# Matrix products that read their moving operand in turns of four columns from each 64-byte line, and a tile of ones 32 bytes lower

## The chip, the cores and the metric

The kernel runs on one core of a Trainium2 chip. The metric is the device time of one execution in microseconds (us), median of the runs shown. Besides these times there is one profiled execution; all rows below come from it.

## The reference

One decoder block in float32 over 256 tokens of width 2048: a mixer with gated linear attention (4 heads) beside multi-scale pooling, merged by sigmoid gates, then cross-attention into 256 memory tokens, then a gated MLP with a depthwise convolution of width 3 (inner width 5632), each on an RMS-normed input and added to the residual stream; at the end a last RMS norm.

```
x = x + hybrid_mixer(rms_norm(x, g_mix), w_in, ..., w_branch, w_out)
x = x + memory_cross_attention(rms_norm(x, g_cross), rms_norm(mem, g_mem), w_cq, w_ckv, w_co)
x = x + conv_glu_ffn(rms_norm(x, g_ffn), w_up, conv_w, conv_b, w_down)
return rms_norm(x, g_final)
```

## The kernel before

**Layout.** Activations lie with features on the 128 partitions and tokens along the free axis. A chunk of 128 features by 256 tokens is held as two float32r parts, the rounded value (hi) and the rest (lo). Class `Act` keeps two chunks in a tile of 4096 bytes per partition: 256 columns hi and 256 columns lo of the first chunk, then the same of the second. `act.both(c)` is the 512 columns of chunk c, `act.hi(c)` its first 256.

**Weights.** They come from DRAM in units (a half unit is up to 1024 columns), and each half is split into hi (`wh`, written by ScalarE) and lo (`wl`, written by VectorE, L110). Both are kept three units ahead of their use.

**Products.** A block of 128 output features is made by `products` from pairs of matmuls into one PSUM tile of 512 columns, 16 pairs in most units:

- L321 multiplies with `wh` all 512 moving columns (hi and lo of the tokens);
- L322 multiplies with `wl` the 256 hi columns and adds into the first half of the same PSUM tile.

Each of the two has a weight load of its own, 128 columns. `total` or `residual` adds the halves of the PSUM tile afterwards. Nearly all products of the kernel go this way: 56 units of `w_in` (tiles ps_k, ps_q, ps_r, ps_g, ps_p), 16 each of `w_branch` (br), `w_out` (ps_wo), the keys (ps_ck), `w_cq` (ps_cq) and `w_co` (ps_wc), 88 of `w_up` (ps_up), 32 of `w_down` with 16 pairs (ps_dn), 10 with 12 pairs (ps_dl), and the first pair of each of the last 6 (ps_dt). That is 56 x 16 + 80 x 16 + 88 x 16 + 32 x 16 + 10 x 12 + 6 = 4222 pairs.

**Other products**, not by `products`: the values and decay inputs at the start (va, L395 to L397), the cross-attention's values (cv, L713 to L715), scores (cs) and outputs (co), and the last six units of `w_down` after their first pair (L912, L913, L918), which read the moving columns as two runs of 128. Plain float32 products stand between: the attention levels (sc, L513), whose moving operand is read in runs of 1, 2, 4, ... up to 64 columns; sums over partitions (cps, L270, one moving column of `ones`); and spreads over partitions with `ones` as the weights (rps, L279, 256 moving columns, and oss, L579, 512).

**Where tiles lie.** The pools follow each other in each partition's memory; two padding pools of 192 and 64 bytes stand around the pool of `wh`. In the built program all `Act` tiles begin at 160 modulo 256 bytes, `wl` at 160, `wh` at 96, `ones` at 192, `ident` at 192.

**Order.** Each engine runs its instructions in the program's order; TensorE's weight loads run beside its matmuls.

Of the kernel before, what the change touches and what calls it, by code (L numbers as in the profile page):

```python
# [8 lines left out]
F32 = mybir.dt.float32  # L9
# [6 lines left out]
P = 128  # L16
T = 256
# [125 lines left out]
def block(ctx, tc, xT, memT, vecs, masks, wa2, wpool, w_va, w_in, w_branch, w_out, w_ckv_k, w_ckv_v, w_cq, w_co, w_up, w_down, out):  # L143
    nc = tc.nc
    PS = bass.MemoryType.PSUM
    const = ctx.enter_context(tc.tile_pool(name="const", bufs=1))
# [63 lines left out]
    nc.sync.dma_start(vec[:, V_CB:], vecs[:, V_CB:])  # L210
    eps_t = const.tile([P, 1], F32, name="eps_t")
    nc.vector.memset(eps_t, EPS)
    ones = const.tile([P, P], F32, name="ones")
    ident = const.tile([P, P], F32, name="ident")
    nc.vector.memset(ones, 1.0)
    make_identity(nc, ident)
    scrap = const.tile([P, 1], F32, name="scrap")
# [5 lines left out]
    pe = {}  # L223
# [83 lines left out]
    def gemm(unit, act, name, n=NC):  # L307

        ps = mm.tile([P, 2 * T], F32, tag="mm", name=f"ps_{name}")
        products(ps, terms(W.get(unit), act, n))  # L310
        return ps

    def terms(wps, act, n):
        return [(wps[2 * k // n], k % (n // 2), act, k) for k in range(n)]

    def products(ps, terms, first=True, last=True):
        for i, ((hi, lo), k, act, c) in enumerate(terms):
            f = first and i == 0
            l = last and i == len(terms) - 1
            wh, wl = hi[:, k * P : (k + 1) * P], lo[:, k * P : (k + 1) * P]  # L320
            nc.tensor.matmul(ps, lhsT=wh, rhs=act.both(c), start=f, stop=False, skip_group_check=True)  # L321
            pe["last"] = nc.tensor.matmul(ps[:, 0:T], lhsT=wl, rhs=act.hi(c), start=False, stop=l, skip_group_check=True)  # L322

    def start_pair(units, act, name, n=NC, between=()):

        wps = [W.get(u) for u in units]
        pss = [mm.tile([P, 2 * T], F32, tag="mm", name=f"ps_{name}{i}") for i in range(2)]
        for half in range(2):
            for i in range(2):
                products(pss[i], terms(wps[i], act, n)[half * n // 2 : (half + 1) * n // 2], first=half == 0, last=half == 1)  # L330
                for f in between[2 * half + i : 2 * half + i + 1]:
                    behind(f)
        return pss
# [318 lines left out]
    for m in range(NC):  # L652
        wps = W.get(br0 + m)
        ys = []
        for n in (1, 0):
            ps = mm.tile([P, 2 * T], F32, tag="mm", name=f"br{m}_{n}")
            products(ps, [(wps[n], k, og if n == 0 else op, k) for k in range(8)])
            y = total(ps, f"br{m}_{n}")
            nc.vector.scalar_tensor_tensor(y, gates[m // 2][:, m % 2, n, :], 1.0, y, ALU.add, ALU.mult)
            ys.append(y)  # L660
        nc.vector.tensor_add(ys[0], ys[0], ys[1])
        nc.scalar.mul(mg.hi(m), ys[0], 0.5)
        nc.vector.scalar_tensor_tensor(mg.lo(m), ys[0], 0.5, mg.hi(m).bitcast(F32), ALU.mult, ALU.subtract)
# [27 lines left out]
    for m in range(NC):  # L691
        ps = gemm(ck0 + m, me, f"ck{m}")
# [10 lines left out]
    for g in range(4):  # L703
        acc = [mm.tile([P, 512], F32, tag="mm", name=f"cv{g}_{t}") for t in range(2)]
        for j in range(4):
            wps = W.get(cv0 + 4 * g + j)
            for k in range(4):
                hi, lo = wps[k // 2]
                wh, wl = hi[:, (k % 2) * 512 : (k % 2 + 1) * 512], lo[:, (k % 2) * 512 : (k % 2 + 1) * 512]
                c = 4 * j + k  # L710
# [82 lines left out]
    last = []  # L793
# [112 lines left out]
    for m in range(NC - TAIL, NC):  # L906
        pool, tag = (aux, "aux") if m >= NC - 2 else (mm, "mm")
        ps = pool.tile([P, 2 * T], F32, tag=tag, name=f"ps_dt{m}")
# [69 lines left out]
```

## Time and profile before

| | |
|---|---|
| time, median of 3 runs | 1702.03 us (1701.56 to 1702.17) |
| time of the profiled execution | 1702.15 us |
| its span, first to last instruction | 1700.4 us |
| TensorE matmuls busy | 1689.0 us, 99% of the span |
| TensorE weight loads busy | 1490.3 us, 88% |
| VectorE, ScalarE busy | 1228.0 us (72%), 897.2 us (53%) |
| mean granted TensorE clock | 0.998 |

Busy time of a matmul includes its way through the array, during which the next has already begun; the pace is therefore read from the starts of successive matmuls, not from their durations.

### The profile page before, as it was taken

The page shows a single profiled execution, that of the slowest core. Times are in us where ns is not written, and L with a number is a line of the kernel's source. Part 1 is how long each engine was busy: PE and PEld are TensorE (multiplying, and loading weights), DVE is VectorE, ACT ScalarE, POOL GpSimd, SP SyncE. Part 2 cuts the span into 40 slices and gives each one's busy share as a digit, 9 for nine tenths or more (in the row PEclk, how much of TensorE's full clock was granted, in tenths as well). Part 3 has the DMA queues.
Part 4 walks back from the last instruction along what each step waited for, and adds up shares of the span by engine and source line. Part 5 has one row for each costly group of instructions (what it writes and reads, how often), then busy time and mean ns, then how long its engine had stood idle before and what let it go on. Part 6 is the DMA issues. An engine that isn't in the chain of part 4 may idle for free.

```text
span 1700.4 us, 25992 instructions
## 1 busy us (share of the span) xinstructions
PE 1689.0 (99%) x9900; PEld 1490.3 (88%) x9900; DVE 1228.0 (72%) x1904; ACT 897.2 (53%) x1376; POOL 31.7 (2%) x137
## 2 busy tenths in 40 slices
PE   9999999999999999999999999999999999999997
PEld 9988988888888888889988888888888888888887
DVE  7687658667889755447777788775677776567776
ACT  7555456445556544445555655553355554345564
POOL 2000000000001000000000000000000000000000
PEclk9999999999999999999999999999999999999999
DMA  8665556556666566655446665666665566665563
GB/s 276 193 204 166 174 161 208 182 169 196 192 218 218 184 191 188 186 186 167 152 148 191 189 190 190 187 186 187 190 190 188 186 187 188 190 191 186 170 178 112
DMA packets 90734, 316.15 MB, mean 186 GB/s; under 512 B 10208, under 2 KB 11104, under 8 KB 90608
## 3 DMA queue, kind: packets, MB, share of 16 engines
q1 hardware_dynamic: 90464, 314.43, 59.4%
q8 instruction: 77, 1.26, 0.3%
q14 instruction: 49, 0.40, 0.1%
q10 hardware_dynamic: 144, 0.05, 0.0%
HBM read 312.35 MB, written 2.10 MB: 185 GB/s over the span
## 4 chain that ended last, share of the span: by engine, by line
PE 99%; DMA 0%; DVE 0%; SPq 0%; ACT 0%; issue 0%; DVEq 0%; ACTq 0%
PE ps_up L321 19%; PE ps_up L322 10%; PE ps_dn L321 7%; PE ps_g L321 7%; PE ps_dn L322 4%; PE ps_ck L321 3%; PE ps_g L322 3%; PE ps_wc L321 3%; PE ps_wo L321 3%; PE ps_cq L321 3%; PE br L321 3%; PE cv L714 2%; PE ps_ck L322 2%; PE cv L713 2%; PE cv L715 2%; PE ps_p L321 2%
## 5 line engine op out<-in xcount | busy, mean ns | idle before, releaser
L110 DVE TENSOR_TENSOR wl<-raw,wh 128x1024 fp32r<-128x1024 f32 (+3 forms) x602 | 718.1, 1194 | 379.4 <-ACT wh L110 371.9
L110 ACT CAST wh<-raw 128x1024 fp32r<-128x1024 f32 (+3 forms) x602 | 614.6, 1023 | 712.2 <-issue 273.2
L321 PE MATMUL ps_up<-h,wh 128*128 128x512 f32 x1408 | 493.0, 395 | 0.0
L322 PE MATMUL ps_up<-h,wl 128*128 128x256 f32 x1408 | 394.8, 280 | 0.0
L321 PEld LDWEIGHTS ps_up<-h,wh 128*128 128x128 f32 x1408 | 264.7, 188 | 61.1
L322 PEld LDWEIGHTS ps_up<-h,wl 128*128 128x128 f32 x1408 | 264.3, 188 | 0.0
L321 PE MATMUL ps_dn<-ga,wh 128*128 128x512 f32 x512 | 179.3, 395 | 0.0
L321 PE MATMUL ps_g<-h,wh 128*128 128x512 f32 x512 | 178.0, 394 | 0.0
L322 PE MATMUL ps_dn<-ga,wl 128*128 128x256 f32 x512 | 143.6, 280 | 0.0
L322 PE MATMUL ps_g<-h,wl 128*128 128x256 f32 x512 | 142.1, 277 | 0.0
L321 PEld LDWEIGHTS ps_dn<-ga,wh 128*128 128x128 f32 x512 | 96.3, 188 | 22.3
L321 PEld LDWEIGHTS ps_g<-h,wh 128*128 128x128 f32 x512 | 96.2, 188 | 20.7 <-ACT wh L110 0.2
L322 PEld LDWEIGHTS ps_g<-h,wl 128*128 128x128 f32 x512 | 96.2, 188 | 0.3 <-issue 0.2
L322 PEld LDWEIGHTS ps_dn<-ga,wl 128*128 128x128 f32 x512 | 96.1, 188 | 0.0
L321 PE MATMUL ps_ck<-me,wh 128*128 128x512 f32 x256 | 89.7, 395 | 0.0
L321 PE MATMUL ps_cq<-h,wh 128*128 128x512 f32 x256 | 87.8, 390 | 0.0
L321 PE MATMUL ps_wc<-oc,wh 128*128 128x512 f32 x256 | 87.6, 390 | 0.0
L321 PE MATMUL ps_wo<-mg,wh 128*128 128x512 f32 x256 | 87.3, 389 | 0.0
L322 PE MATMUL ps_ck<-me,wl 128*128 128x256 f32 x256 | 71.7, 280 | 0.0
L322 PE MATMUL ps_cq<-h,wl 128*128 128x256 f32 x256 | 70.7, 276 | 0.0
L322 PE MATMUL ps_wc<-oc,wl 128*128 128x256 f32 x256 | 70.5, 276 | 0.0
L322 PE MATMUL ps_wo<-mg,wl 128*128 128x256 f32 x256 | 70.5, 276 | 0.0
(321 smaller groups left out, 2765.5 us busy)
## 6 DMA issues: line engine op xcount, KB each, us to landing
raw<-w_up SPq DMA_DIRECT2D x176, 512.0 KB, 3.6
raw<-w_in SPq DMA_DIRECT2D x112, 512.0 KB, 3.9
raw<-w_down SPq DMA_DIRECT2D x64, 512.0 KB, 3.6
raw<-w_branch SPq DMA_DIRECT2D x32, 512.0 KB, 4.4
raw<-w_out SPq DMA_DIRECT2D x32, 512.0 KB, 4.4
raw<-w_ckv_k SPq DMA_DIRECT2D x32, 512.0 KB, 3.7
raw<-w_ckv_v SPq DMA_DIRECT2D x32, 512.0 KB, 3.5
raw<-w_cq SPq DMA_DIRECT2D x32, 512.0 KB, 4.3
```

The source lines that it names most:

```text
L110: return self.nc.scalar.copy(hi, src), self.nc.vector.tensor_sub(lo, src, hi.bitcast(F32))
L321: nc.tensor.matmul(ps, lhsT=wh, rhs=act.both(c), start=f, stop=False, skip_group_check=True)
L322: pe["last"] = nc.tensor.matmul(ps[:, 0:T], lhsT=wl, rhs=act.hi(c), start=False, stop=l, skip_group_check=True)
L713: nc.tensor.matmul(acc[t], lhsT=xh, rhs=wh, start=c == 0, stop=False)
L714: nc.tensor.matmul(acc[t], lhsT=xh, rhs=wl, start=False, stop=False)
L715: nc.tensor.matmul(acc[t], lhsT=xl, rhs=wh, start=False, stop=c == NC - 1)
```

## The change

`products` hands both matmuls views of the same memory in another order. `fours` splits the 512 (or 256) columns into 64-byte lines of 16 columns, and each line into four groups of four columns. The matmul goes first through the first group of every line, then the second group of every line, and so on: four columns (16 bytes), a jump of 64 bytes from group start to group start, 32 (or 16) groups in one turn, four turns. PSUM is written in the same order, so each result lands where it did.

The second part puts a gap of 224 bytes ahead of `ones` and one of 32 bytes behind it. `ones` then begins at 160 modulo 256, everything behind it moves by 256 bytes, so all other tiles keep their place modulo 256.

```
+    gaps = [const.tile([P, 56], F32, name="gap0")]
     ones = const.tile([P, P], F32, name="ones")
+    gaps.append(const.tile([P, 8], F32, name="gap1"))
     ident = const.tile([P, P], F32, name="ident")
+    for gap in gaps:
+        nc.vector.memset(gap, 0.0)
...
+    def fours(ap):
+
+        return ap.rearrange("p (l u e) -> p u l e", u=4, e=4)
+
     def products(ps, terms, first=True, last=True):
...
-            nc.tensor.matmul(ps, lhsT=wh, rhs=act.both(c), start=f, stop=False, skip_group_check=True)
-            pe["last"] = nc.tensor.matmul(ps[:, 0:T], lhsT=wl, rhs=act.hi(c), start=False, stop=l, skip_group_check=True)
+            nc.tensor.matmul(fours(ps), lhsT=wh, rhs=fours(act.both(c)), start=f, stop=False, skip_group_check=True)
+            pe["last"] = nc.tensor.matmul(fours(ps[:, 0:T]), lhsT=wl, rhs=fours(act.hi(c)), start=False, stop=l, skip_group_check=True)
```

No instruction changes its place on any engine. On TensorE the 4222 x 2 matmuls of `products` have the shape 128x4x32x4 in place of 128x512, or 128x4x16x4 in place of 128x256; VectorE has two small memsets more.

## Rows read from the trace of the kernel before

**Rows 1.** The page: span, busy time, clock and DMA by slices, chain by engine.

```profile
span 1700.4 us, 25992 instructions
...
PE 1689.0 (99%) x9900; PEld 1490.3 (88%) x9900; DVE 1228.0 (72%) x1904; ACT 897.2 (53%) x1376; POOL 31.7 (2%) x137
...
PEclk9999999999999999999999999999999999999999
DMA  8665556556666566655446665666665566665563
...
PE 99%; DMA 0%; DVE 0%; SPq 0%; ACT 0%; issue 0%; DVEq 0%; ACTq 0%
```

**Rows 2.** Timeline of TensorE, queries of the cross-attention: start, duration, instruction.

```profile
800.11 0.39 PE L321 MATMUL ps_cq<-h,wh 128*128 128x512 f32 x1
800.34 0.28 PE L322 MATMUL ps_cq<-h,wl 128*128 128x256 f32 x1
800.45 0.39 PE L321 MATMUL ps_cq<-h,wh 128*128 128x512 f32 x1
800.68 0.28 PE L322 MATMUL ps_cq<-h,wl 128*128 128x256 f32 x1
800.79 0.39 PE L321 MATMUL ps_cq<-h,wh 128*128 128x512 f32 x1
```

**Rows 3.** Timeline of TensorE, the MLP's first product.

```profile
1000.05 0.40 PE L321 MATMUL ps_up<-h,wh 128*128 128x512 f32 x1
1000.28 0.28 PE L322 MATMUL ps_up<-h,wl 128*128 128x256 f32 x1
1000.40 0.40 PE L321 MATMUL ps_up<-h,wh 128*128 128x512 f32 x1
```

**Rows 4.** Windows: length; busy (instructions) of PE, PEld, DVE, ACT, POOL; clock, DMA share, GB/s.

```profile
251.00:323.00 72.00, 72.00 (x414) 63.00 (x413) 54.42 (x87) 41.92 (x63) 0.25 (x2) 1.00 0.63 198
...
395.00:570.00 175.00, 174.99 (x1030) 154.52 (x1029) 152.00 (x238) 103.50 (x176) 11.99 (x14) 1.00 0.64 205
583.00:660.00 77.00, 77.00 (x443) 67.47 (x441) 44.75 (x57) 31.82 (x40) 0.00 (x0) 1.00 0.61 188
962.00:1623.00 661.00, 661.00 (x3778) 578.75 (x3778) 489.61 (x734) 342.24 (x496) 8.63 (x86) 1.00 0.61 186
```

**Rows 5.** Timeline of TensorE around the spread of the norms in the keys.

```profile
580.75 0.39 PE L321 MATMUL ps_ck<-me,wh 128*128 128x512 f32 x1
...
581.09 0.39 PE L321 MATMUL ps_ck<-me,wh 128*128 128x512 f32 x1
581.32 0.28 PE L322 MATMUL ps_ck<-me,wl 128*128 128x256 f32 x1
581.43 0.59 PE L279 MATMUL rps_mem<-diag_mem,ones 128*128 128x256 f32 x2
581.87 0.59 PE L279 MATMUL rps_wo<-diag_wo,ones 128*128 128x256 f32 x2
...
582.65 0.40 PE L321 MATMUL ps_ck<-me,wh 128*128 128x512 f32 x1
...
583.00 0.40 PE L321 MATMUL ps_ck<-me,wh 128*128 128x512 f32 x1
```

**Rows 6.** The chain that ended last, in order of time: start, length, what.

```profile
120.67 1.73 PE sc L513 x16
...
196.87 1.73 PE sc L513 x16
...
248.61 1.72 PE oss L579 x4
323.13 1.73 PE pps L616 x8
...
961.98 0.43 PE rps_wc L279 x2
1629.51 0.57 PE ps_dl L321 x2
```

**Rows 7.** Timeline of TensorE, scores of the cross-attention.

```profile
860.09 0.28 PE L742 MATMUL cs<-ka,qa 128*128 128x256 f32 x1
860.21 0.28 PE L740 MATMUL cs<-ka,qa 128*128 128x256 f32 x1
860.33 0.28 PE L741 MATMUL cs<-ka,qa 128*128 128x256 f32 x1
```

**Rows 8.** Timeline of TensorE, sums over partitions, one moving column each.

```profile
575.07 0.50 PE L270 MATMUL cps_mem<-ones,acc_mem 128*128 128x1 f32 x4
575.43 0.58 PE L270 MATMUL cps_wo<-ones,acc_wo 128*128 128x1 f32 x4
575.88 0.47 PE L321 MATMUL ps_ck<-me,wh 128*128 128x512 f32 x1
```

**Rows 9.** Timeline of TensorE, the last units of the MLP's second product.

```profile
1670.63 0.28 PE L912 MATMUL ps_dt<-ga,wl 128*128 128x256 f32 x1
1670.75 0.28 PE L913 MATMUL ps_dt<-ga,wh 128*128 128x256 f32 x1
1670.87 0.28 PE L912 MATMUL ps_dt<-ga,wl 128*128 128x256 f32 x1
```

## Prediction

> **What bounds the kernel now.** The page comes first. TensorE is busy for 99% of the span, the chain that ended last is TensorE for 99%, and its granted clock is full in every slice [rows 1]. Nothing else has to become quicker for a gain, and nothing is late: what counts is the pace of the matmuls themselves.
>
> That pace is read from the timeline, from start to start. In the cross-attention's queries a pair of `products` begins every 0.34 us: 0.23 for the 512 columns, 0.11 for the 256 [rows 2]. In the MLP it is 0.35: 0.23 and 0.12 [rows 3]. At the granted clock of 1.00, which is 2.4 GHz, 768 columns are 768 / 2.4 = 320 ns. So each pair loses 20 or 30 ns, with nothing waited for.
>
> The windows show that these are two settled paces. From 395 to 570 us 515 pairs take 175 us, 0.340 each; from 962 to 1623 us 1889 pairs take 661 us, 0.350 each; the windows at 251 and 583 give 0.348 [rows 4]. Same instructions, same shapes, same clock, two paces. What switches them is seen in the keys: pairs at 0.34, then four plain float32 records with `ones` as the weights, and from there on pairs at 0.35 [rows 5]. The chain names the other two such places and their ends [rows 6]: the spread of the attention norms at 248.61 (with `ones`), until the pooling products at 323.13; the spread for the MLP at 961.98, until two products wait at 1629.51. So the longer pace holds 72.8 us from 250.3 to 323.1, 78.3 us from 582.6 to the end of the keys near 661, and 667.1 us from 962.4 to 1629.5: 818 us, or 818 / 0.350 = 2338 of the 4222 pairs.
>
> I read this as two streams of one engine that fall into step. While the moving columns of one matmul run, the weights of the next are loaded from the same memory, and how the two stand to each other decides the loss. Three rows bear this out. Scores of 256 moving columns, with moving operand and weights both at 160 modulo 256, take 0.12 each [rows 7], though the 256 columns of a pair with the next `wh` at 96 take 0.11 at the better pace: same columns, other offsets. Products with one moving column stand 0.81 us for eight records, 0.10 each [rows 8]: that is about what a weight load alone costs, so a 256-column matmul cannot go below it. And plain float32 products, which take the moving columns at half the rate, lose next to nothing: two records with 256 columns take 0.44 us [rows 5], 0.22 each for 512 steps, of which 512 / 2.4 = 0.213.
>
> The Trainium skill, "TensorE: Matmul & The Clock Gate", Part 2, step 1, says the two read ports are independent and loading the next weights takes nothing from the running matmul. By that, the two paces should not exist; the rows above differ, and the measurement decides.
>
> **The change, part by part.** *Tile of ones at 160.* `ones` stands at 192, half a 64-byte line beside the weights of `products` (96 and 160). If the longer pace is entered through `ones` for that reason, `ones` at 160 leaves the pairs at the shorter pace: 2338 x (350 - 340) = 23.4 us. Lower bound: nothing, if any float32 spread sets the longer pace. The matmuls with `ones` themselves are a handful of microseconds and keep theirs.
>
> *The turns, number of instructions.* 4222 pairs before and after, in the same order; weight loads unchanged; no wait added; no DMA moved. VectorE's two small memsets lie at the start, where TensorE still waits for the first weights; they cost nothing I can see.
>
> *The turns, pace.* No row shows a matmul that reads four columns and jumps, at full rate. Bounds: the best is columns alone, 320 ns a pair, and with the rows for the undisturbed case (about 215 for 512 steps, 110 for the weight load under the 256) 325 to 327. The worst that the nearest rows give is one lost step for each piece. At 0.34 a pair is 816 clocks for 768 columns, which is 17 for each 16: as if each 64-byte line cost one. If each group of four cost one, it would be 5 for 4, 960 clocks, 400 ns. What shows short runs is the attention levels: their moving operand goes in runs of 1 to 64 columns, yet each level takes 1.73 us for 16 records, the first and the last alike [rows 6]; but 64 columns at half rate hide under the weight load's 0.11, so this only says that a jump is not dear there. Two runs of 128 cost as much as one of 256, 0.12 and 0.12 [rows 9].
>
> I take a gain, near the undisturbed end. In order, the moving columns go through a 64-byte line in 16 clocks and keep the same neighbourhood to the weight load for long; in turns they leave a line after four, so the two meet often and briefly rather than for a stretch. Of the 20 ns lost at the shorter pace the undisturbed rows explain 5 to 7; of the other 13 I let the turns remove 9: 331 ns a pair. That share is a choice between the ends.
>
> **Sum.** 4222 x (340 - 331) = 38.0 us, and 23.4 us from the pairs now at 350: 61.4 us. Against the profiled execution's 1702.15 us (span 1700.4 and 1.75 around it; the median is 1702.03) that gives 1640.7, say **1641 us**.
>
> *Cover.* Where TensorE speeds up by 3 to 6%, the others must follow. Between 395 and 570 us VectorE is busy 152 of 175 [rows 4], 87%, and would be 89% at 331 ns; ScalarE stands at 104. In the MLP VectorE has 490 of 661. DMA is at 0.64 at most. So nothing else becomes the bound; if the weights' split were late in the branches, it would be late by a part of the 5 us gained there.
>
> **The rivals.**
>
> *Only the ones count.* The turns leave the 17 clocks for 16 as they are, and all pairs run at 340: 1702.15 - 23.4 = 1679. For it: 544 and 272 clocks at the better pace are in proportion to the columns, as a loss of the moving stream alone would be. Against: 256 columns with other weights lose twice as much [rows 7].
>
> *Neither counts.* The paces are set by something else, the float32 spread itself, and the turns run as before: 1702.
>
> *The poorer step everywhere.* With turns the two streams always fall into the longer pace: the other 1884 pairs lose 10 ns each, 18.8 us: 1721. With the 0.12 and twice that of the scores it would be 360 a pair and 1702 + 1884 x 20 + 2338 x 10 = 1763.
>
> *A jump costs a clock.* On the other side outright: 960 clocks a pair, 1702 + 1884 x 60 + 2338 x 50 = 1932. It decides early: the ones give 23.4 us / 4222 = 5.5 ns a pair on average, and a pair has 192 groups of four, so 0.03 ns more for each group eats it. For it: the 17 for 16. Against: the same count of lines costs once 0.11 and once 0.12, so most of the loss is not the line's.
>
> The Trainium skill speaks for this last rival: "PSUM — Partial Sum Buffer", Specifications, gives PSUM cachelines of 8 bytes and says any access pattern that is not contiguous slows matmuls significantly. The turns write PSUM in pieces of 16 bytes. It gives no size; no row here writes PSUM in such pieces. "SBUF — State Buffer", Specifications, asks for at least two hits in each 16-byte line, which groups of four float32 columns meet.
>
> **How the numbers follow.** Gain of the turns, alone or with the ones (1615 to 1665): 0.45. Only the ones (1665 to 1695): 0.20. Neither: 0.06. Poorer step (1705 to 1763): 0.12. A jump costs (beyond): 0.17. The predicted time is the first case's. About 0.2%, 3.4 us, is what a measurement of this kernel tells from no change: faster 0.65, within 0.06, slower 0.29. The range runs from 1615 (325 ns a pair) to 1721 (all pairs at 350); it leaves out the jump's cost and the dearer part of the poorer step. The likeliest case's own range is 1615 to 1665.
>
> **What the profile would show.** Starts of L329 and L330 (the same two matmuls) in the queries every 0.33 us in place of 0.34, in the MLP the same 0.33, no step at the spreads with `ones`. The windows' share of VectorE should rise. If the queries stay at 0.34 and the MLP comes down to 0.34, only the ones counted. If pairs take 0.36 or more in every stage, the jumps or the meeting of the two streams cost more than the order in line did, and the sign is wrong. If the two paces remain, the reading of the ones is wrong.

## The result: faster by 1.4%, where 3.6% was forecast

The changed kernel takes 1677.74 us (median, 1677.48 to 1679.01) beside 1702.1 us of the kernel before: a ratio of 0.9858, 95% interval 0.9841 to 0.9875. That is 24.4 us less; the forecast was 61.4 us less, 1641 us. The sign and the range (1615 to 1721) held; the size did not.

The page of the changed kernel: span, busy time by engine, granted clock, and the chain that ended last by engine. These lines answer to [rows 1].

```profile
span 1675.7 us, 25994 instructions
...
PE 1663.7 (99%) x9900; PEld 1480.0 (88%) x9900; DVE 1228.0 (73%) x1906; ACT 899.2 (54%) x1376; POOL 31.5 (2%) x137
...
PEclk9999999999999999999999999999999999999999
...
PE 98%; DVE 1%; DMA 0%; issue 0%; SPq 0%; ACT 0%; DVEq 0%; ACTq 0%
```

TensorE is still the bound, its clock is still full (0.998 on average), VectorE's work is the same to a tenth of a microsecond. Nearly all of the 24.7 us of span, 24.3, came off the pace of the pairs. Where, the windows say; they have the columns of [rows 4].

```profile
251.00:323.00 72.00, 72.00 (x423) 63.92 (x422) 55.55 (x90) 42.63 (x65) 0.25 (x2) 1.00 0.63 205
395.00:570.00 175.00, 174.99 (x1030) 155.18 (x1029) 153.16 (x240) 104.88 (x178) 12.95 (x15) 1.00 0.64 205
583.00:660.00 77.00, 77.00 (x447) 67.97 (x446) 45.64 (x57) 33.17 (x42) 0.00 (x0) 1.00 0.63 195
```

From 395 to 570 us 1030 matmuls ran before and 1030 run now: the pairs that stood at 0.340 us stand there still. The window at 251 us holds 423 matmuls in place of 414. Start by start, the MLP and the keys after their spread with `ones` (timeline of TensorE; [rows 3] and [rows 5] are the same places):

```profile
999.95 0.39 PE L329 MATMUL ps_up<-h,wh 128*128 128x512 f32 x1
1000.18 0.28 PE L330 MATMUL ps_up<-h,wl 128*128 128x256 f32 x1
1000.29 0.39 PE L329 MATMUL ps_up<-h,wh 128*128 128x512 f32 x1
1000.52 0.28 PE L330 MATMUL ps_up<-h,wl 128*128 128x256 f32 x1
1000.63 0.39 PE L329 MATMUL ps_up<-h,wh 128*128 128x512 f32 x1
```

```profile
577.95 0.59 PE L283 MATMUL rps_mem<-diag_mem,ones 128*128 128x256 f32 x2
578.38 0.59 PE L283 MATMUL rps_wo<-diag_wo,ones 128*128 128x256 f32 x2
...
579.14 0.39 PE L329 MATMUL ps_ck<-me,wh 128*128 128x512 f32 x1
...
579.49 0.39 PE L329 MATMUL ps_ck<-me,wh 128*128 128x512 f32 x1
...
579.83 0.39 PE L329 MATMUL ps_ck<-me,wh 128*128 128x512 f32 x1
```

A pair begins every 0.34 us where it was 0.35, and after the spread the pace stays. Taken from the starts of all pairs, the median is 340 ns in every stage, 225 for the 512 columns and 115 for the 256; the kernel before had 227 and 113 (or 226 and 114) at its shorter pace, 233 and 117 at its longer. The sum over the pairs is 1438.0 us where it was 1462.3, 24.3 less: 2338 pairs by 10 ns is 23.4. So the pairs at 350 came down to 340, and the pairs at 340 did not move.

### The profile page after: what moved, and what is told of

It is laid out like the page before. It is cut to its first block, busy times and chain, and to the rows that moved or that the text cites. A ratio compares the mean times of both kernels' runs of the same rounds, so it can differ in the third digit from the quotient of the medians.

```text
span 1675.7 us, 25994 instructions
## 1 busy us (share of the span) xinstructions
PE 1663.7 (99%) x9900; PEld 1480.0 (88%) x9900; DVE 1228.0 (73%) x1906; ACT 899.2 (54%) x1376; POOL 31.5 (2%) x137
## 4 chain that ended last, share of the span: by engine, by line
PE 98%; DVE 1%; DMA 0%; issue 0%; SPq 0%; ACT 0%; DVEq 0%; ACTq 0%
PE ps_up L329 19%; PE ps_up L330 10%; PE ps_g L329 7%; PE ps_dn L329 7%; PE ps_g L330 4%; PE ps_dn L330 4%; PE ps_wo L329 3%; PE ps_wc L329 3%; PE ps_cq L329 3%; PE ps_ck L329 3%; PE br L329 3%; PE cv L722 2%; PE cv L721 2%; PE cv L723 2%; PE ps_cq L330 2%; PE ps_wc L330 2%
## 5 line engine op out<-in xcount | busy, mean ns | idle before, releaser
L329 PE MATMUL ps_up<-h,wh 128*128 128x512 f32 x1408 | 479.2, 385 | 0.0
L330 PE MATMUL ps_up<-h,wl 128*128 128x256 f32 x1408 | 387.2, 275 | 0.0
L329 PE MATMUL ps_dn<-ga,wh 128*128 128x512 f32 x512 | 174.2, 385 | 0.0
```

Of the source, the lines that this page charges most:

```text
L329: nc.tensor.matmul(fours(ps), lhsT=wh, rhs=fours(act.both(c)), start=f, stop=False, skip_group_check=True)
L330: pe["last"] = nc.tensor.matmul(fours(ps[:, 0:T]), lhsT=wl, rhs=fours(act.hi(c)), start=False, stop=l, skip_group_check=True)
```

## The experiments

In what follows the pace of a stage is the median distance from the start of one pair's first matmul to that of the next, in ns, taken from the trace's starts; "the 512" and "the 256" are the two matmuls of a pair. The edits are shown against the changed kernel, cut at "...".

### One part alone

The turns without the move of the ones:

```
-    gaps = [const.tile([P, 56], F32, name="gap0")]
+    gaps = [const.tile([P, 64], F32, name="gap0")]
     ones = const.tile([P, P], F32, name="ones")
-    gaps.append(const.tile([P, 8], F32, name="gap1"))
```

> The turns of the changed kernel with the tile of ones back at 192 modulo 256. Theory T (the turns themselves bring every pair to 0.340 us, whatever the phase that a float32 spread leaves): 340 ns in the keys after the spread, in the MLP and elsewhere, 1678 us. Rival O (the place of the ones does it): the MLP falls back to about 0.350 and the time to about 1700 us.

Measured: 1677.76 us, ratio 0.9860 (0.9844 to 0.9877). All of the gain is there with `ones` back at 192. The MLP's timeline:

```profile
999.91 0.39 PE L328 MATMUL ps_up<-h,wh 128*128 128x512 f32 x1
...
1000.25 0.39 PE L328 MATMUL ps_up<-h,wh 128*128 128x512 f32 x1
...
1000.60 0.39 PE L328 MATMUL ps_up<-h,wh 128*128 128x512 f32 x1
```

This kernel and the changed one differ in the place of `ones` alone, and a trace of that is left. Between the sums over partitions (`cps`) and the spread, in the keys from 573.6 us and ahead of the MLP from 951.8, 12 pairs each stand at 346 or 347 ns here, and at 340 in the changed kernel. Behind the spreads both run at 340.

The move of the ones without the turns:

```
-            nc.tensor.matmul(fours(ps), lhsT=wh, rhs=fours(act.both(c)), ...)
+            nc.tensor.matmul(ps, lhsT=wh, rhs=act.both(c), ...)
...
```

> Moving columns and PSUM in line as before, only the tile of ones at 160. Rival O: the pairs stay at 0.340 after each spread with ones, 1678 us. Theory T: still 0.350 from 251 to 323, 583 to 661 and 962 to 1629 us, 1702 us.

Measured: 1679.0 us, ratio 0.9864 (0.9849 to 0.9879). The same gain again, in line, and without the longer pace after any spread with `ones`:

```profile
1000.01 0.39 PE L329 MATMUL ps_up<-h,wh 128*128 128x512 f32 x1
...
1000.35 0.39 PE L329 MATMUL ps_up<-h,wh 128*128 128x512 f32 x1
...
1000.69 0.39 PE L329 MATMUL ps_up<-h,wh 128*128 128x512 f32 x1
```

Both theories were half right, and their gains don't add. Either edit takes the same 10 ns off the same pairs, and nothing is left for the other. 2338 x 10 = 23.4 us stood in the prediction for the ones alone, and 22.9 were measured for them. Against the kernel before, this edit also moves every tile behind `ones` by 256 bytes and adds two memsets; no run in line has that move with `ones` left where it was, so that the place of `ones` does it is likely, not shown.

### Is it the read or PSUM?

One side in turns and the other in line, by stage (`turns` is `fours` with its two numbers as arguments):

```
+    FORMS = {'krq': ((4, 4), None), 'gp': (None, (4, 4)), ..., 'up': ((4, 4), None), 'dn': (None, (4, 4)), ...}
...
+            nc.tensor.matmul(turns(ps, form["write"]), lhsT=wh, rhs=turns(act.both(c), form["read"]), ...)
```

> By stage, either only the moving read goes in turns (keys, queries and gates r of the mixer, branches, keys of the cross-attention, its output product, the MLP's first product) or only PSUM is written in turns (gates and pooling inputs, the mixer's output product, the queries of the cross-attention, the MLP's second product); columns then land in other tokens' places, so the values are not the reference's. If the two streams from the one memory set the pace, stages with the read in turns run at 340 ns like the changed kernel, and stages with only PSUM in turns at 340 or 350 like the kernel before. If PSUM's order matters by itself, the PSUM stages stand apart from both, above 350 if pieces of 16 bytes cost there.

Measured: 1678.36 us, one run. Every stage has 340. Where the read goes in turns (q, branches, keys, the MLP's first product) a pair is 225 + 115, as in the changed kernel; where only PSUM does (gates, wo, cq, the second product) it is 226 or 227 + 114 or 113, as in line. How a pair splits goes with the read alone; PSUM's order leaves no trace in the time. `ones` lies at 160 here, where the order in line runs at 340 too, so this run doesn't say which of the two sides takes the 10 ns off with `ones` at 192.

### Other turns

> Other turns by stage, read and PSUM alike (pieces x pitch in bytes): w_in 32x64, branches 8x64, wo 16x32, keys 16x128, cq 16x256, wc 32x256, MLP first 64x256, second 32x128, last units 8x64. If a turn only sets which step the two streams fall into, each stage sits at a multiple of 16 clocks: 333, 340 or 347 ns. If each jump costs by itself, 8-byte pieces are dearer than 16-byte pieces by a fixed amount for 192 more jumps, and 64-byte pieces come near the order in line.

> The dear turns split into read and PSUM (columns land in other tokens' places where only one goes in turns): 8 bytes from each 64, read only (k, q, r), PSUM only (gates, pooling); 16 from each 256, read only (branches), PSUM only (wo); 16 from each 32, read only (ck), PSUM only (cq); 16 from each 128, read only (wc); 32 from each 128 (MLP first) and 64 from each 128 (second), read and PSUM. If all of the price is the read's, the PSUM stages run at 340 ns. If PSUM in pieces that are not contiguous is what costs, the dear stages are the PSUM ones.

> Other orders by stage, read and PSUM alike: turns of 16x64 bytes for the 512 columns only (k, q, r) or for the 256 only (gates, pooling); 32x128 for both (branches); 32x128 for the 512 and 16x64 for the 256 (wo); pieces taken by turns from the two halves of the columns, of 32 bytes (ck), 16 bytes (MLP first), 64 bytes (MLP second), 128 bytes (last units); from the four quarters, 16 bytes (wc); 128x256 turns (cq). If 17 clocks for 16 columns is what the moving read takes at best, no order comes below 340 ns on average, and the ones with a jump after each piece lie above it. If the loss is the order's, some order comes to 333 or below.

The edits are other numbers in the same table, and in the third another view:

```
+    FORMS = {'krq': ((2, 8), (2, 8)), ..., 'br': ((8, 2), (8, 2)), ..., 'up': ((4, 16), (4, 16)), ...}
...
+        if f and f[0] == "alt":
+            return ap.rearrange("p (u l e) -> p l u e", u=f[1], e=f[2])
```

Measured: 1874.57, 1801.73 and 1768.83 us, one run each, none near the changed kernel. By stage, bytes in a piece x distance to the next; the last units in `turn_sizes` went 8 x 32, not the 8 x 64 of the text above (a line of 4 x 2 columns is 32 bytes):

| read | pair, ns | PSUM alone in that order, ns |
|---|---|---|
| in line | 340 or 350 | |
| 16 x 64 (the change) | 340 | 340 |
| 16 x 32 | 353 | 340 |
| 16 x 128 | 365 | |
| 16 x 256 | 415 | 350 |
| 32 x 64 | 349 to 351 | |
| 32 x 128 | 340 (going round between 332 and 352) | |
| 32 x 256 | 358 (363 on average) | |
| 64 x 128, 64 x 256 | 360 | |
| 128 x 256 | 355 | |
| 8 x 32 | 693 | |
| 8 x 64 | 650 | 340 |
| 16, 32, 64, 128 bytes by turns from two halves | 377, 367, 360, 354 | |
| 16 bytes by turns from four quarters | 400 (403 on average) | |

The gates and pooling inputs with only the 256 in turns, and wo with 32 x 128 for the 512 and 16 x 64 for the 256 (both in `other_orders`), stand at 340.

The dearest turns that were split into read and PSUM, 8 bytes from each 64, only read so (first three lines) and only written so in PSUM (last three), timeline of the split run:

```profile
119.95 0.61 PE L334 MATMUL ps_q<-h,wh 128*128 128x512 f32 x1
120.38 0.40 PE L335 MATMUL ps_q<-h,wl 128*128 128x256 f32 x1
120.60 0.61 PE L334 MATMUL ps_q<-h,wh 128*128 128x512 f32 x1
...
300.10 0.39 PE L334 MATMUL ps_g<-h,wh 128*128 128x512 f32 x1
300.33 0.28 PE L335 MATMUL ps_g<-h,wl 128*128 128x256 f32 x1
300.44 0.39 PE L334 MATMUL ps_g<-h,wh 128*128 128x512 f32 x1
```

The price is all the read's: 0.65 us a pair in one stage, 0.34 in the other. The other dear turns cost the same with PSUM in line as with PSUM in turns: 353 for 16 x 32, 365 for 16 x 128, 415 for 16 x 256. It is no fixed price for a jump either: 16-byte pieces cost 340 at a distance of 64 bytes, more both nearer and farther. The 350 of wo with only PSUM in turns of 16 x 256 looks like the longer pace of the order in line (232 + 118 beside 233 + 117); a price of that PSUM order itself isn't ruled out, since no other stage had it with the read in line. That `ones` isn't the only way into the longer pace the keys at the start show: in the kernel before and in `line_ones160` alike, 14 pairs from 62.3 us stand at 350, behind a product that reads `ident`, in a stretch that the prediction didn't count.

In `other_orders` the mixer's queries, with the 512 in turns and the 256 in line, went round 329, 336 and 348 ns, 337.6 on average, below 340 for once; its keys and r had the same form and mixed that cycle with 347. As a kernel of its own:

```
-            pe["last"] = nc.tensor.matmul(fours(ps[:, 0:T]), lhsT=wl, rhs=fours(act.hi(c)), ...)
+            pe["last"] = nc.tensor.matmul(ps[:, 0:T], lhsT=wl, rhs=act.hi(c), ...)
```

> The changed kernel with turns for the 512 columns only and the 256 in line. If the cycle of 329, 336 and 348 ns seen in the queries holds in the long stretches, pairs average 338 ns and the time is about 1670 us; if the 347 ns seen in parts of r holds there, about 1705 us. Theory of the steps that an entry chooses: each stretch is one or the other from its start on.

Measured: 1699.11 us, ratio 0.9981 (0.9972 to 0.9991) to the kernel before. Both paces of that form lasted: wo and wc went round the cycle, 338 on average, while the branches and the MLP fell into the other pace, 346.7 ns from 964 to 1624 us:

```profile
1000.12 0.39 PE L329 MATMUL ps_up<-h,wh 128*128 128x512 f32 x1
1000.35 0.28 PE L330 MATMUL ps_up<-h,wl 128*128 128x256 f32 x1
1000.47 0.39 PE L329 MATMUL ps_up<-h,wh 128*128 128x512 f32 x1
```

### Places of the weights, entries, alignment

The high weights at another place modulo 256 bytes in each stage, in line and in turns:

```
+                hi = self.his.tile([P, off + half], F32R, tag="wh", ..., padded_shape=[P, UNIT + 64])[:, off : off + half]
```

> Order in line, ones at 160, and the high weights at another place modulo 256 in each stage (96 before): k, q, r 128; gates 160; pooling inputs and branches 192; wo 224; ck 0; cq 32; wc 64; MLP first 128, 224, 32 by thirds, second 160, 0, 192. If the remaining 20 ns of a pair are the meeting of moving columns and weight load, the pace changes with the place, at best towards 327 ns and at worst to 350 or above. If they belong to the moving stream alone, 340 stays at every place.

> The same places of the high weights by stage, with the turns of the changed kernel. If turns make the pace independent of how the two streams stand to each other, 340 ns at every place. If they only fall into another of several steps, some places give 333 or 347.

Measured: 1718.89 and 1685.71 us, one run each. In line no other place keeps the 340 of the old one: stage medians are 347 to 353, means 346.7 to 353.4. With the weights at 224, in the MLP:

```profile
1299.85 0.40 PE L391 MATMUL ps_up<-h,wh 128*128 128x512 f32 x1
...
1300.21 0.40 PE L391 MATMUL ps_up<-h,wh 128*128 128x512 f32 x1
...
1300.56 0.40 PE L391 MATMUL ps_up<-h,wh 128*128 128x512 f32 x1
```

In turns, in the same stages at the same places, means are 340.0 to 346.7 and most pairs scatter from 332 to 356. So the turns make the pace care less where the weights lie; they don't bring it below 340.

A small float32 product with `ones` ahead of every third unit pair of the MLP, each with other moving columns:

```
+        nc.tensor.matmul(ps[:, 0:cols], lhsT=ones, rhs=ones[:, at : at + (cols - 1) * step + 1 : step], start=True, stop=True)
```

> The changed kernel with one small float32 product (weights ones, another start, count or step of moving columns each time) ahead of every third unit pair of the MLP's first product: 14 restarts. If the pace of a pair is a step that the entry chooses and that then lasts, the stretches behind the restarts stand at 333, 340 or 347 ns, each for 96 pairs or more. If turns always lead to 340, all 14 stretches come back to 340 within a few pairs; the time is then 1678 us and some 10 us for the restarts.

Measured: 1682.55 us, one run. All 14 stretches come back to 340 within five pairs, so these entries choose nothing. But from 485.8 to 572.9 us, where this kernel does nothing other than the changed one, 252 pairs in a row stand at 346.7, where the changed kernel had 340:

```profile
520.17 0.39 PE L329 MATMUL ps_wo<-mg,wh 128*128 128x512 f32 x1
520.40 0.28 PE L330 MATMUL ps_wo<-mg,wl 128*128 128x256 f32 x1
520.51 0.39 PE L329 MATMUL ps_wo<-mg,wh 128*128 128x512 f32 x1
520.74 0.28 PE L330 MATMUL ps_wo<-mg,wl 128*128 128x256 f32 x1
520.86 0.39 PE L329 MATMUL ps_wo<-mg,wh 128*128 128x512 f32 x1
```

Just before, at 484.2 us here and 483.9 in the changed kernel, two 512s run in a row and then two 256s; out of that same place one execution goes on at 340 and the other at 346.7. TensorE's instructions up to there are the same in the same order, so they alone don't settle the pace. The changed kernel itself has some 30 pairs at 333 from 121.8 us, 28 at 347 from 160.3 and 26 at 333 from 186.6. So turns have several lasting paces as well, 333, 340 and 347; 340 is the one that most entries lead to.

Every tile 32 bytes further, order in line or in turns by stage:

```
-    gaps = [const.tile([P, 56], F32, name="gap0")]
+    gaps = [const.tile([P, 64], F32, name="gap0")]
+    FORMS = {'krq': (None, None), ..., 'br': ((4, 4), (4, 4)), ..., 'up': (None, None), 'dn': ((4, 4), (4, 4)), ...}
```

> Every tile 32 bytes further, so that moving columns and low weights begin on a 64-byte line (192 modulo 256; high weights 128, ones 192), in turns in branches, ck, wc and the MLP's second product, in line elsewhere. If the loss depends only on how the tiles stand to each other, 340 ns in both orders as with ones at 160. If it is the 64-byte line that a misaligned stream crosses once more, the pair comes down.

Measured: 1678.83 us, one run, 340 in every stage in both orders. As long as the tiles keep their distances, where the moving columns begin within a 64-byte line doesn't matter. `ones` lies at 192 here, and the MLP's first product, in line behind a spread with it, stays at 340. So 192 by itself isn't the way into the longer pace; here it is a whole number of 64-byte lines from the weights at 128 and 192, where before it was half a line beside those at 96 and 160.

### Which stream loses the 20 ns?

Weights of 64 and of 32 columns in place of 128 (32 where it says 64):

```
+            nh, nl = (64 if i and x in form["halved"] else P for x in "hl")
+            nc.tensor.matmul(turns(ps[0:nh], form["write"]), lhsT=wh[:, 0:nh], rhs=turns(act.both(c), form["read"]), ...)
```

> Weight loads of 64 columns in place of 128 from the second pair of each accumulation on, so that half the output features are left out: in line with only the low weights halved (k, q, r), only the high (gates, pooling), both (branches, MLP first, last units), none (wc); in turns with low (wo), high (ck), both (cq, MLP second). If the weight load costs the moving stream its 20 ns, a pair with both halved loses about half of it, 330 ns or less, and the 512 and the 256 can be told apart by which load runs beside them. If the moving stream alone loses them, 340 ns stays, in line and in turns.

> Weight loads of 32 columns in place of 128 from the second pair on, so that three quarters of the output features are left out: in line with both narrowed (k, q, r; wo; MLP first), only low (gates, pooling), only high (branches); in turns with both (ck; MLP second), only low (cq), only high (wc). If the weight load costs the moving stream 20 ns a pair, both narrowed give about 325 ns. If the loss belongs to the moving stream, 340 stays.

Measured: 1683.36 and 1698.08 us, one run each. A weight load of 128 columns takes 188 ns in the profile, of 64 columns 134, of 32 columns 107. With both loads halved in turns a pair is 336 or 337 (MLP second, cq), in line 341 or 340 (branches, MLP first; 344 and 342 on average); with both at a quarter 341 in turns, 344 to 350 in line. With one load of the two shortened, stages lie between 334 and 347. The MLP's second product with both at a quarter, in turns:

```profile
1160.18 0.38 PE L337 MATMUL ps_dn<-ga,wh 128*32 128x512 f32 x1
...
1160.51 0.39 PE L337 MATMUL ps_dn<-ga,wh 128*32 128x512 f32 x1
...
1160.85 0.39 PE L337 MATMUL ps_dn<-ga,wh 128*32 128x512 f32 x1
```

Three quarters of the weight columns gone, and the loss is still there or larger. So the loss doesn't shrink with the weight load's length; that the pace moves at all, by 4 ns down to 10 up, says that the loads do act on it.

Operands that stand still in memory:

```
+        return ap[:, None, 0:n].to_broadcast([P, ap.shape[1] // n, n]) if n else ap
...
+        return ap[:, 0:1].to_broadcast([P, P]) if form["still"] else ap
```

> Operands that stand still in memory (values are then not the reference's): the moving operand is the same 4 columns again and again (k, q, r; MLP first), the same 16 (wo) or 64 (ck); the weights are one column 128 times (gates, pooling; cq; MLP second); both, with 4 columns (branches) or 16 (wc). If the lost 20 ns come from moving columns and weight load meeting in memory, a pair drops towards 325 ns with either standing still. If the moving read alone loses them on its way from line to line, only the stages with still columns drop. If neither, 340 stays everywhere.

Measured: 1681.64 us, one run. The MLP's first product with the same four columns read again and again:

```profile
1000.06 0.38 PE L343 MATMUL ps_up<-h,wh 128*128 128x512 f32 x1
1000.28 0.28 PE L344 MATMUL ps_up<-h,wl 128*128 128x256 f32 x1
1000.39 0.38 PE L343 MATMUL ps_up<-h,wh 128*128 128x512 f32 x1
1000.61 0.28 PE L344 MATMUL ps_up<-h,wl 128*128 128x256 f32 x1
1000.72 0.38 PE L343 MATMUL ps_up<-h,wh 128*128 128x512 f32 x1
```

| moving columns | weights | pair, ns (512 + 256) |
|---|---|---|
| the same 4 | as ever | 330 (217 + 113) |
| the same 4 | one column, still | 330 (217 + 113) |
| the same 16 | as ever, or still | 365 |
| the same 64 | as ever | 340 |
| in line | one column, still | 350 (340 to 352, 347 or 348 on average) |

The MLP's second product, moving columns in line and the weights one column read again and again:

```profile
1160.13 0.39 PE L343 MATMUL ps_dn<-ga,wh 128*128 128x512 f32 x1
...
1160.48 0.40 PE L343 MATMUL ps_dn<-ga,wh 128*128 128x512 f32 x1
...
1160.83 0.39 PE L343 MATMUL ps_dn<-ga,wh 128*128 128x512 f32 x1
```

Here the streams part. As soon as the moving read stays on one piece of 16 bytes, the pair is 330 to the nanosecond, whether the weights go on or stand still; when the weights stand still and the moving read goes on, nothing is won. So 10 of the 20 ns come with the moving read's way through memory, and 10 stay without it. It isn't shown that they are the moving read's alone: weights that stand still are still read, 128 times at one place, and a moving read that stays on 16 bytes may meet the weights' read less often. Standing still on 64 bytes is dearer than going on, 365, so the way's price isn't one per line.

## Why the prediction was wrong

**The bound** was right: TensorE's pace, nothing late; the chain is TensorE for 98%. The cover held too: in `still_reads`, with the branches at 330 ns a pair, TensorE is busy without a break from 400 to 475 us and VectorE is busy 66.7 of those 75 us, the 89% that were forecast for 331.

**The two paces and their size** were right. The three stretches, 2338 pairs, 10 ns each: 23.4 us forecast for the ones, 22.9 measured for the edit that moves them. That the place of `ones` is the way in fits that run, and the 12 pairs at 347 of `turns_ones192`; it isn't separated from the move of all tiles behind. The reason given, half a 64-byte line beside the weights, fits the 340 of `all_32_bytes_on`, where every tile moved with `ones`; no other distance was tried.

**The turns' term failed.** The step is "of the other 13 I let the turns remove 9: 331 ns a pair", 38.0 us. It measured nothing: the median stays at 340 in every stage, and the pairs sum to 1438.0 us with both edits and to 1439.0 with the ones alone, 1.0 us for the 38.0. The sum counted the 10 ns of the longer pace once, as the ones' gain. That the turns give those 10 ns as well it didn't foresee, but that leaves the total as it is; what was missing is the 9 ns below 340. The size was a choice between ends, and the runs show it near the floor: 330 is what a pair costs when the moving read doesn't move at all, above the 325 to 327 that stood as the best. With whole weights no order that really reads its columns came below 337.6 on average over a stage.

**The picture behind it isn't borne out.** I argued that moving columns and the load of the next weights get in each other's way, and that turns, which make them meet briefly, leave less of the loss. The place of the weights does change the pace in line, as [rows 7] suggested, so the two streams act on each other. But shorter loads, and weights that stand still, don't take the loss away, and a moving read that stands still takes it to 330. Half of the loss goes with the moving read's steps; whether through the weights' read or by itself stays open. One reading of a row was off by a little: the products of one moving column stand 111 or 112 ns apart in the trace, not 0.10 us [rows 8].

**The rivals.** "Only the ones count" named the right time, 1679, and the right pairs, but not the reason: the turns alone do the same. The sign given for it, queries at 0.34 and the MLP down to 0.34, came, and couldn't tell the two edits apart. "The poorer step everywhere" and "a jump costs a clock" were wrong for this turn; that jumps can cost is so for its neighbours: 16 bytes each 128 or 256 and 8 bytes each 64 cost 365, 415 and 650, though not by one price for each jump. The Trainium skill, "PSUM — Partial Sum Buffer", Specifications, which spoke for that rival, differs from the trace: pieces of 8 and of 16 bytes in PSUM ran at 340 (one stage, 16 x 256, at 350, which may be the longer pace of the order in line). The Trainium skill, "SBUF — State Buffer", Specifications, asks two hits of each 16-byte line for full bandwidth. The read of 8-byte pieces has two and cost 650; four hits cost 340 to 415 by the distance.

**What stays open:** what makes 340 and 350 (or 333, 340 and 347) lasting paces, whether and why the place of `ones` leads into one, why the turns take the pairs at 350 to 340, why 64 bytes is the distance at which 16-byte pieces cost no more than the order in line, and whether some order keeps 333. Why a still read of 64 bytes takes 365 stays open too.

## What to carry to other kernels

When two edits are meant to remove losses of the same instructions, run each alone before adding their terms; here each gave all of the gain. Where matmuls run back to back with nothing waited for, look at the distance between their starts by stage: two paces for the same shapes are a state that something enters, and an edit of a few lines that moves one tile was worth as much here as reordering every read. The order in which moving columns are read can double the time (650 and 693 ns a pair for 340); the order in which PSUM is written did not matter here, one stage left open.

## What the hardware showed that I had not expected

- Same instructions at full clock have lasting paces that differ by 2 to 4%: 340 and 350 in line, 333, 340 and 347 in turns; a pace held for 1900 pairs. What ran before has a part in it, but the same instructions in the same order went on at 340 in one execution and at 346.7 in another.
- The moving read's order is worth a factor of two: 340 ns a pair for 16 bytes each 64, 415 for 16 each 256, 650 for 8 each 64, 693 for 8 each 32; in PSUM pieces of 8 each 64 were free.
- A moving read that stays on 16 bytes takes 217 and 113 ns for 512 and 256 columns; 512 / 2.4 and 256 / 2.4 are 213.3 and 106.7. The 113 barely exceeds the 111 or 112 that products of one column take. With both loads at half the columns, in turns, the 256 took 108 to 116, 112 or 113 in the median, so it isn't shown that the load's length holds it at 113.
